# A two-layer f32 trunk on one core: all five engines in written order, seven split weight blocks, and a k-tile-major start

## The chip, the cores and the metric

The kernel runs on one core of one Trainium2 chip. The metric is the device time of one execution in microseconds, the median of several runs.

## The reference

The reference is a trunk of two layers over one sequence of 256 tokens with 1024 features, all in float32. Layer 0 mixes tokens by latent attention (MLA), layer 1 by forgetting attention (FoX). Cut to what matters:

```python
h = x
for i in range(2):
    h = h + 0.5 * swiglu(rms_norm(h, ffn_norm[i, 0]), ffn_w_in[i, 0], ffn_w_out[i, 0])
    u = rms_norm(h, mix_norm[i])
    h = h + (mla_mixer(u, ...) if i == 0 else fox_mixer(u, ...))
    h = h + 0.5 * swiglu(rms_norm(h, ffn_norm[i, 1]), ffn_w_in[i, 1], ffn_w_out[i, 1])
    gate = sigmoid(rms_norm(h, ple_norm[i]) @ ple_w_gate[i])
    h = h + gate * (p[i] @ ple_w_proj[i])
return rms_norm(h, final_norm)

def swiglu(x, w_in, w_out):          # w_in (1024, 2 * 2816), w_out (2816, 1024)
    gate, up = split(x @ w_in, 2, axis=-1)
    return (silu(gate) * up) @ w_out
```

## The kernel before, in words

Activations lie transposed: hT holds 1024 features as 8 k-tiles of 128 partitions by 256 tokens. Every large product is done in three reduced-precision products: each f32 operand is split into a high half and a low half (hi, lo), and hi·hi, lo·hi and hi·lo are summed. For a k-tile, PE runs one matmul with 512 columns (weight hi against activation hi and lo side by side, L228) and one with 256 (weight lo against activation hi, L229). Such a couple is called a pair in this text.

Weights come in blocks of 128 by 1024 (512 KB), one DMA each on SyncE's queue, into a buffer `raw`. For each half of 512 columns ScalarE writes `whi` (L97) and VectorE, in some stages POOL, subtracts to get `wlo` (L99). The class `Weights` keeps a plan of all blocks in order of use. `RAW`, `PAIRS` and `AHEAD` are the number of raw buffers, of split blocks, and how far the splits run ahead: 6, 5 and 4.

A `Norm` makes the operand of the next stage from hT: `scaled` writes the high half u on ScalarE (L270) and the low half on VectorE (L271), `square` and POOL's sum (L288) collect the norm's squares. The factor of each token comes later: `by_token` sums squares on PE (`pst`, L301), VectorE writes v (L304), POOL raises it to the power -0.5 (`rtok`, L306), VectorE multiplies the identity by it (`dg`, L311); `by_column` spreads it by a product (`pb`, L315), which ScalarE copies to `rb` (L317).

An FFN has 22 chunks of 128 hidden features. For each, a gate block (`pg`) and an up block (`pu`) of eight k-tiles go through PE; VectorE takes each out of PSUM times rb (`two`, L328), POOL adds its two halves (`gu`, L330), ScalarE does the silu (`sg`), POOL multiplies (`hid`, L334), and ScalarE and VectorE split that to `hs` (L208, L209). Then come eight output columns of 22 k-tiles each (`po`), and VectorE adds them to hT (L364). In the attentions, `fill` and `finish` interleave the output projection's columns (`ps`) with the last heads; the first four columns wait for the last head together, and `finish` adds a column to hT (L443) and hands it to the next norm. In FoX, POOL adds the halves of each projected query and key (L637). The position tables for MLA (`tables`, 41 small VectorE operations and two sines) are made during the first FFN. `ple` is the gated embedding at the end of each layer.

Seven PSUM banks are shared by all these products and one is kept for the norms.

The order of work: on PE and SyncE the instructions run in the order in which the program writes them. On the other three engines a planner orders them when the kernel is built, from its own costs and due times; on the chip each engine then runs its list in order, waiting at its head.

Of the kernel before, what the change touches and what calls it, by code (L numbers as in the profile page):

```python
# [61 lines left out]
class Weights:  # L62


    RAW, PAIRS, AHEAD = 6, 5, 4

    def __init__(self, nc, pool, plan, shared):
        self.nc, self.pool, self.plan = nc, pool, plan
        self.shared = shared
        self.got = self.loaded = self.fetched = 0  # L70
        self.live, self.raws, self.pairs = [], {}, {}

    def fetch(self):
# [6 lines left out]
    def load(self, pieces=1, between=None):  # L80
        nc = self.nc
        if pieces > 1:
            raw, src = self.fetch()
        else:
            while self.fetched < min(len(self.plan), self.loaded + self.RAW):
                nc.sync.dma_start(*self.fetch())
            raw = self.raws.pop(self.loaded)
        n = raw.shape[-1]
        hi = self.pool.tile([P, n], F32R, name="whi", bufs=self.PAIRS)
        lo = self.pool.tile([P, n], F32R, name="wlo", bufs=self.PAIRS)  # L90
        for i in range(pieces):
            c = slice(i * n // pieces, (i + 1) * n // pieces)
            if pieces > 1:
                nc.sync.dma_start(raw[:, c], src[:, c])
            for b in range(c.start, c.stop, 512):
                b = slice(b, min(b + 512, c.stop))
                nc.scalar.activation(hi[:, b], raw[:, b], AF.Copy)  # L97
                eng = nc.gpsimd if b.start and self.loaded in self.shared else nc.vector
                eng.tensor_sub(lo[:, b], raw[:, b], hi[:, b].bitcast(F32))  # L99
            if between:  # L100
                between(i)
        self.pairs[self.loaded] = (hi, lo)
        self.loaded += 1

    def ahead(self):
        oldest = min(self.live, default=self.got)
        while self.loaded < min(len(self.plan), self.got + self.AHEAD, oldest + self.PAIRS):
            self.load()

    def get(self, n=1):  # L110

        ids = list(range(self.got, self.got + n))
        self.got += n
        self.live += ids
        while self.loaded < self.got:
            self.load()
        self.ahead()
        return [(i, *self.pairs.pop(i)) for i in ids]

    def done(self, *ws):  # L120
        for w in ws:
            self.live.remove(w[0])
        self.ahead()
# [3 lines left out]
def trunk(ctx, tc, xT, pT, pos, gains, freq, bf, ffn_in, ffn_out, w_down, w_uq, w_ukv, mla_o,  # L127
# [13 lines left out]
    def plan_ffn(i):  # L141
        plan.extend(ffn_in[i, c] for c in range(2 * KF))
# [55 lines left out]
    def tmp(name):  # L198
        return work.tile([P, T], F32, name=name, tag="tmp", bufs=7)
# [54 lines left out]
    class Norm:  # L254
# [8 lines left out]
        def scaled(self, b, src, vector=False, cuts=(slice(0, T),)):  # L263
            g = g_sb[:, self.gain + b:self.gain + b + 1]
            hi, lo = self.pair[:, 0, b, :], self.pair[:, 1, b, :]
            for c in cuts:
                if vector:
                    nc.vector.tensor_scalar(hi[:, c], src[:, c], g, None, op0=ALU.mult)
                else:
                    nc.scalar.activation(hi[:, c], src[:, c], AF.Copy, scale=g)  # L270
                nc.vector.scalar_tensor_tensor(lo[:, c], src[:, c], g, hi[:, c].bitcast(F32),  # L271
                                               op0=ALU.mult, op1=ALU.subtract)

        def square(self, src, pool=False, cuts=(slice(0, T),)):
# [16 lines left out]
        def block(self, b, src, cuts=(slice(0, T),)):  # L291
            if self.gain is not None:
                self.scaled(b, src, cuts=cuts)
            self.square(src, cuts=cuts)

        def by_token(self, columns=True):
# [10 lines left out]
            if not columns:  # L307
                return
            self.dg = work.tile([P, 2, P], F32, name="dg", bufs=2)
            for t in range(2):  # L310
                nc.vector.tensor_scalar(self.dg[:, t, :], ident, self.rtok[:, t:t + 1], None, op0=ALU.mult)  # L311

        def by_column(self):
            pb = psm.tile([P, T], F32, name="pb", tag="small")
            nc.tensor.matmul(pb, ones, self.dg.rearrange("p a b -> p (a b)"), start=True, stop=True)  # L315
# [5 lines left out]
    def ffn(norm, nxt, meanwhile=None, at=1):  # L321
        hs = big.tile([P, 2, KF, T], F32R, name="hs", tag="big")

        def gate_up(c, ps):
            gu = []
            for p in ps:
                two = work.tile([P, 2, T], F32, name="two", tag="pair2", bufs=5)
                nc.vector.tensor_mul(two, p, norm.rb2)  # L328
                gu.append(tmp("gu"))
                nc.gpsimd.tensor_add(gu[-1], two[:, 0, :], two[:, 1, :])  # L330
            sg = tmp("sg")
            nc.scalar.activation(sg, gu[0], AF.Silu)  # L332
            hid = tmp("hid")
            nc.gpsimd.tensor_mul(hid, sg, gu[1])  # L334
            split(hs[:, 0, c, :], hs[:, 1, c, :], hid)

        ps0 = bank("pg"), bank("pu")
        blocks(ps0, norm.pair)
        waits = [(0, ps0)]
        for c in range(1, KF):  # L340
            pg = bank("pg")
            block(pg, norm.pair)
            if c == at:
                norm.by_token()
            pu = bank("pu")
# [3 lines left out]
            waits.append((c, (pg, pu)))  # L349
            if c >= at:  # L350
                for w in waits:
                    gate_up(*w)
                waits = []
            if c == 4 and meanwhile:
                meanwhile()
# [12 lines left out]
    def attention(project, score, v, scale, nxt, lag, fills, early, cumq=None):  # L368
# [4 lines left out]
        def scores(h):  # L373
# [15 lines left out]
            pr = work.tile([P, 3 * P], F32, name="pr", bufs=5)  # L389
            den = work.tile([P, 2], F32, name="den", bufs=3)  # L390
            nc.scalar.activation(pr[:, :P], ps[:, :P], AF.Exp, bias=nm[:, 0:1], scale=by[0], accum_out=den[:, 0:1])
            nc.scalar.activation(pr[:, P:], ps[:, P:], AF.Exp, bias=nm[:, 1:2], scale=by[1], accum_out=den[:, 1:2])
            inv = work.tile([P, 2], F32, name="inv", bufs=3)
# [3 lines left out]
            probs[h] = pr  # L397

        def turn(h):
            pr = probs.pop(h)  # L400
# [39 lines left out]
        def finish(d):  # L440
            W.done(ws[d])
            for p in parts(pss[d]):
                nc.vector.tensor_add(hT[:, d, :], p, hT[:, d, :])  # L443
            nxt.block(d, hT[:, d, :])

        for h in range(H + lag):
            if h < H:
# [8 lines left out]
            if h < H:  # L456
                project(h, 1)
            fill_some(fills.get((h, 1), 0))
# [17 lines left out]
    def mla(norm, nxt):  # L476
# [4 lines left out]
        norm.by_token()  # L481
        block(pkv, norm.pair, norm.by_column)
        nq = Norm(G_Q, 2, 2 * P, tag="q")
        for s in range(2):
            cq = tmp("cq")
            nc.vector.tensor_mul(cq, pq[s], norm.rb)
            nq.block(s, cq)
        nkv = Norm(G_KV, 1, P, tag="kv")
        ckv = tmp("ckv")
        nc.vector.tensor_mul(ckv, pkv, norm.rb)  # L490
        nkv.block(0, ckv)
# [424 lines left out]
```

## Time and profile before

| | |
|---|---|
| median of three runs | 1041.34 us (1040.74 to 1042.61) |
| profiled execution | 1040.49 us |
| span of its trace | 1038.7 us |
| granted clock of TensorE, mean | 0.991 |
| PE busy | 1003.6 us, 97% |
| VectorE (DVE) busy | 811.8 us, 78% |
| ScalarE (ACT) busy | 549.3 us, 53% |
| POOL busy | 409.3 us, 39% |
| DMA | 179.05 MB, mean 172 GB/s |

The span runs from the first to the last instruction; the execution's own time is 1.8 us longer. "Busy" is the share of the span in which an engine had an instruction in work; a matmul's end is modelled, so a busy PE can still run below its pace. In the list of waits, each row names the waiting instruction, the one that released it, the total in us, how often and the longest. In the list of groups, after the count stand busy us and the mean ns of one instruction, then the idle time ahead. A row of the table by stretches holds the busy time of PE, PEld, DVE, ACT and POOL with their counts of instructions, then the clock, the DMA share and GB/s. A row of the order of events holds start us, duration us, engine, line and what was made from what; in brackets the idle time before it and who ended it.

### The profile page before, as it was taken

To read this page: it belongs to the slowest core of one execution; us is meant where nothing else is said; L and a number is where in the kernel's file an instruction comes from. 1 tells how busy PE (TensorE), PEld (TensorE's weight loads), DVE (VectorE), ACT (ScalarE), POOL (GpSimd) and SP (SyncE) were. 2 spreads that over 40 slices of the span, in tenths; PEclk is the share of its full clock that TensorE was granted. 3 is DMA by queue.
4 is the path that set the end of the run, shared out by engine and by line. 5 is a ranking of instruction groups with operands and counts; after the bars stand their busy time and mean duration, and the time that the engine had idled before them with its cause. 6 is when DMAs were issued, how large, how long until landed. Compare 5 with 4: busy or idle time off the path is not lost. (4 is left out here: it accounts for less than half of the span.)

```text
span 1038.7 us, 17058 instructions
## 1 busy us (share of the span) xinstructions
PE 1003.6 (97%) x6084; PEld 888.0 (85%) x6084; DVE 811.8 (78%) x1367; ACT 549.3 (53%) x1168; POOL 409.3 (39%) x422
## 2 busy tenths in 40 slices
PE   6999999999979999999999999999999799999997
PEld 4888888987868888889888888899888688888896
DVE  8899987576669999766889997765766699997764
ACT  4445555466545554545655555556545455555554
POOL 4629531361326545110255552113664265551102
PEclk9999999999989999999999999999999899999998
DMA  7555666641345665665556656664443456656631
GB/s 274 186 195 159 187 205 199 204 143 61 92 158 180 201 184 185 193 198 166 187 177 202 186 179 181 196 207 149 143 152 113 161 169 198 193 180 194 195 119 42
DMA packets 51973, 179.05 MB, mean 172 GB/s; under 512 B 6064, under 2 KB 6960, under 8 KB 51888
## 3 DMA queue, kind: packets, MB, share of 16 engines
q1 hardware_dynamic: 50880, 176.48, 53.9%
q10 hardware_dynamic: 1008, 1.48, 0.4%
q8 instruction: 48, 0.79, 0.3%
q14 instruction: 37, 0.30, 0.1%
HBM read 176.89 MB, written 1.05 MB: 171 GB/s over the span
## 5 line engine op out<-in xcount | busy, mean ns | idle before, releaser
L99 DVE TENSOR_TENSOR wlo<-raw,whi 128x512 fp32r<-128x512 f32 (+1 forms) x646 | 472.3, 766 | 100.4 <-ACT whi L97 99.3
L97 ACT ACTIVATE whi<-raw 128x512 fp32r<-128x512 f32 (+1 forms) x688 | 382.7, 608 | 235.6 <-issue 81.9
L228 PE MATMUL pg<-u,whi 128*128 128x512 f32 x704 | 255.0, 400 | 20.0 <-DVE u L271 20.0
L228 PE MATMUL pu<-u,whi 128*128 128x512 f32 x704 | 254.3, 399 | 0.0
L330 POOL TENSOR_TENSOR gu<-two 128x256 f32<-128x256 f32 x176 | 169.0, 965 | 182.1 <-DVE two L328 165.8
L228 PE MATMUL po<-hs,whi 128*128 128x512 f32 x616 | 215.2, 393 | 0.9 <-DVE hs L209 0.9
L229 PE MATMUL pg<-u,wlo 128*128 128x256 f32 x704 | 199.9, 284 | 1.5 <-DVE wlo L99 1.5
L229 PE MATMUL pu<-u,wlo 128*128 128x256 f32 x704 | 199.9, 284 | 0.5 <-DVE wlo L99 0.5
L228 PEld LDWEIGHTS pg<-u,whi 128*128 128x128 f32 x704 | 133.4, 189 | 52.9 <-DVE u L271 14.8
L229 PE MATMUL po<-hs,wlo 128*128 128x256 f32 x616 | 173.3, 281 | 0.0
L228 PEld LDWEIGHTS pu<-u,whi 128*128 128x128 f32 x704 | 134.6, 191 | 30.7
L228 PEld LDWEIGHTS po<-hs,whi 128*128 128x128 f32 x616 | 115.7, 188 | 27.4 <-DVE hs L209 1.2
L229 PEld LDWEIGHTS pg<-u,wlo 128*128 128x128 f32 x704 | 133.7, 190 | 3.5 <-DVE wlo L99 3.4
L229 PEld LDWEIGHTS pu<-u,wlo 128*128 128x128 f32 x704 | 134.7, 191 | 1.0 <-DVE wlo L99 1.0
L208 ACT ACTIVATE hs<-hid 128x256 fp32r<-128x256 f32 x88 | 36.8, 418 | 165.3 <-POOL hid L334 165.3
L288 POOL TENSOR_TENSOR acc<-acc,sq 128x256 f32<-128x256 f32 x53 | 46.4, 876 | 187.3 <-ACT sq L280 186.6
L229 PEld LDWEIGHTS po<-hs,wlo 128*128 128x128 f32 x616 | 115.8, 188 | 0.0
L334 POOL TENSOR_TENSOR hid<-sg,gu 128x256 f32<-128x256 f32 x88 | 90.3, 1026 | 24.5 <-ACT sg L332 17.1
L99 POOL TENSOR_TENSOR wlo<-raw,whi 128x512 fp32r<-128x512 f32 x42 | 58.4, 1396 | 64.6 <-ACT whi L97 64.4
L209 DVE TENSOR_TENSOR hs<-hid,hs 128x256 fp32r<-128x256 f32 x88 | 58.7, 667 | 22.9 <-ACT hs L208 20.9
L328 DVE TENSOR_TENSOR two<-pg,rb 128x512 f32<-128x512 f32 x88 | 60.1, 683 | 8.7 <-PE pg L229 8.7
L328 DVE TENSOR_TENSOR two<-pu,rb 128x512 f32<-128x512 f32 x88 | 59.7, 678 | 0.3
(223 smaller groups left out, 1370.9 us busy)
## 6 DMA issues: line engine op xcount, KB each, us to landing
raw<-in_ffn_in_dram SPq DMA_DIRECT2D x174, 512.0 KB, 3.6
raw<-in_ffn_out_dram SPq DMA_DIRECT2D x64, 512.0 KB, 3.5
raw<-in_ffn_out_dram SPq DMA_DIRECT2D x32, 384.0 KB, 3.2
raw<-in_ple_gate_dram SPq DMA_DIRECT2D x16, 512.0 KB, 3.6
raw<-in_fox_qk_dram SPq DMA_DIRECT2D x16, 512.0 KB, 3.5
raw<-in_mla_o_dram SPq DMA_DIRECT2D x8, 512.0 KB, 3.5
raw<-in_fox_o_dram SPq DMA_DIRECT2D x8, 512.0 KB, 3.5
raw<-in_fox_v_dram SPq DMA_DIRECT2D x6, 512.0 KB, 3.4
```

Source lines behind the costliest of these rows:

```text
L97: nc.scalar.activation(hi[:, b], raw[:, b], AF.Copy)
L99: eng.tensor_sub(lo[:, b], raw[:, b], hi[:, b].bitcast(F32))
L208: nc.scalar.activation(hi, src, AF.Copy)
L209: nc.vector.tensor_sub(lo, src, hi.bitcast(F32))
L228: nc.tensor.matmul(ps, hi, x[:, :, k, :], start=k == 0, stop=False)
L229: nc.tensor.matmul(ps[:, 1, :], lo, x[:, 0, k, :], start=False, stop=k == last)
L288: nc.gpsimd.tensor_add(new, self.acc, sq)
L328: nc.vector.tensor_mul(two, p, norm.rb2)
L330: nc.gpsimd.tensor_add(gu[-1], two[:, 0, :], two[:, 1, :])
L334: nc.gpsimd.tensor_mul(hid, sg, gu[1])
```

## The change

All five engines run in the order in which the program writes them (`manual_schedule()` without a list), and the program is rewritten for that. Weight splits are written out at chosen places by `pump`, `catch_up` and `get`: ScalarE runs up to two blocks ahead of VectorE, and a block is split by one 1024-wide instruction per engine, or by two halves on VectorE and POOL for blocks in `shared`. There are seven split blocks and four raw ones, instead of five and six. The work of `Norm.block` is parted into `high`, `low` and `square`, with `last` for the last column, whose high half is made on VectorE. `dg` is gone: rtok, broadcast along its columns, is PE's weight and the identity its operand. The first four blocks of the first FFN come from a new array `ffn_first` by k-tiles: a slab has two k-tiles of all four blocks. Ahead of them PE runs 16 dummy products of zeros. The position tables are a generator that gives one step per half chunk of the first FFN. The `hs` split of a chunk follows the gate of the next chunk. In FoX the halves of a key are added on VectorE. The embedding's input is loaded and split during the FFN before it. `tmp` has 5 buffers instead of 7, `pair2` 4 instead of 5, `pr` 4 instead of 5.

```diff
-    RAW, PAIRS, AHEAD = 6, 5, 4
+    RAW, PAIRS = 4, 7
...
+    def fetch(self):
+        while self.fetched < min(len(self.plan), self.loaded + self.RAW):
+            self.nc.sync.dma_start(*self.raw())
...
+    def high(self, i, c):
+        self.nc.scalar.activation(self.pairs[i][0][:, c], self.raws[i][:, c], AF.Copy)
+
+    def low(self, i, c, eng=None):
+        hi, lo = self.pairs[i]
+        (eng or self.nc.vector).tensor_sub(lo[:, c], self.raws[i][:, c], hi[:, c].bitcast(F32))
+
+    def begin(self):
+        if self.begun < min(len(self.plan), min(self.live, default=self.got) + self.PAIRS):
+            hi, _ = self.pair()
+            self.high(self.begun - 1, slice(0, hi.shape[-1]))
+            return True
+
+    def pump(self, n=1):
+        for _ in range(n):
+            while self.begun < self.loaded + 2 and self.begin():
+                pass
+            if self.loaded == self.begun:
+                return
+            i = self.loaded
+            w = self.plan[i].shape[-1]
+            cut = 512 if i in self.shared else w
+            self.low(i, slice(0, cut))
+            if cut < w:
+                self.low(i, slice(cut, w), self.nc.gpsimd)
+            del self.raws[i]
+            self.loaded += 1
+            self.fetch()
+
+    def catch_up(self):
+        if self.loaded < self.got + self.PAIRS - 3:
+            self.pump()
...
+        def last(self, b, src):
+            self.high(b, src, True)
+            self.low(b, src)
+            self.square(src)
...
-            self.dg = work.tile([P, 2, P], F32, name="dg", bufs=2)
-            for t in range(2):
-                nc.vector.tensor_scalar(self.dg[:, t, :], ident, self.rtok[:, t:t + 1], None, op0=ALU.mult)
 
         def by_column(self):
             pb = psm.tile([P, T], F32, name="pb", tag="small")
-            nc.tensor.matmul(pb, ones, self.dg.rearrange("p a b -> p (a b)"), start=True, stop=True)
+            for t in range(2):
+                nc.tensor.matmul(pb[:, t * P:(t + 1) * P], self.rtok[:, t:t + 1].to_broadcast([P, P]), ident,
+                                 start=True, stop=True)
...
+        def gate(c, ps, pumps=1):
+            evacuate(c, 0, ps)
+            W.pump(pumps)
+            if c:
+                hidden(c - 1)
             sg = tmp("sg")
+            nc.scalar.activation(sg, gu.pop((c, 0)), AF.Silu)
+            gu[c, 0] = sg
+            next(meanwhile, None)
+
+        def up(c, ps, pumps=1):
+            evacuate(c, 1, ps)
+            hid[c] = tmp("hid")
+            nc.gpsimd.tensor_mul(hid[c], gu.pop((c, 0)), gu.pop((c, 1)))
+            W.pump(pumps)
+            if c % 2:
+                W.catch_up()
+            next(meanwhile, None)
...
+                for x, ps in enumerate(waits):
+                    gate(x, ps[0], x)
+                    up(x, ps[1], 0)
+                gate(c, pg)
+            up(c, pu, c > at)
         for d in range(KD):
...
+                if a + KD < KF:
+                    W.pump()
+                    next(meanwhile, None)
+                    if d == a == 0:
+                        hidden(KF - 1)
...
         def finish(d):
             W.done(ws[d])
+            src = hT[:, d, :]
             for p in parts(pss[d]):
-                nc.vector.tensor_add(hT[:, d, :], p, hT[:, d, :])
-            nxt.block(d, hT[:, d, :])
+                nc.vector.tensor_add(src, p, src)
+            if d == KD - 1:
+                nxt.last(d, src)
+                W.pump()
+                return
+            nxt.high(d, src)
+            if d < early and d:
+                nxt.low(d - 1, hT[:, d - 1, :])
+            if d >= early - 1:
+                W.pump()
+                nxt.low(d, src)
+            nxt.square(src)
...
-            nc.gpsimd.tensor_add(kq[:, 2 * h + half, :], two[:, 0, :], two[:, 1, :])
+            (nc.vector if half else nc.gpsimd).tensor_add(kq[:, 2 * h + half, :], two[:, 0, :], two[:, 1, :])
+            W.pump()
...
+    warm = const.tile([P, T], BF16, name="warm")
+    nc.vector.memset(warm, 0.0)
+    cold = bank("cold", (P, T))
+    for _ in range(16):
+        nc.tensor.matmul(cold, warm[:, :P], warm, start=True, stop=True)
+    for k in range(KD):
+        if k % 2 == 0:
+            W.pair()
+        n0.high(k, hT[:, k, :])
+        W.high(k // 2, half[k % 2])
+        n0.low(k, hT[:, k, :])
+        W.low(k // 2, half[k % 2])
+        n0.square(hT[:, k, :], pool=k % 2 == 1)
+        if k % 2:
+            W.loaded += 1
+
+    def first(ps):
+        W.fetch()
+        for k in range(0, KD, 2):
+            w, = W.get()
+            for j in range(2):
+                for i, p in enumerate(ps):
+                    part(p, w, n0.pair, range(k + j, k + j + 1), KD - 1, at=lambda x: (j * 4 + i) * P)
+            W.done(w)
+            W.pump()
...
-        with tc.manual_schedule(engines={mybir.EngineType.PE, mybir.EngineType.SP}):
+        with tc.manual_schedule():
```

In the embedding, `gated` makes the low half of the column before and pumps once between the sigmoid's input and the product with the gate. In MLA, the pumps stand behind `by_token`, behind `cr` (two), behind `turned`, behind each second half of `queries`, and behind the values (two).

More of the change, by code (lines that the diff above doesn't have):

```diff
@@ L78, in fetch @@
         return raw, src
[L80 to L108, printed above, removed]
+    def fetch(self):
+        while self.fetched < min(len(self.plan), self.loaded + self.RAW):
+            self.nc.sync.dma_start(*self.raw())
+    def pair(self):
+        n = self.plan[self.begun].shape[-1]
+        self.pairs[self.begun] = [self.pool.tile([P, n], F32R, name=x, bufs=self.PAIRS) for x in ("whi", "wlo")]
+        self.begun += 1
+        return self.pairs[self.begun - 1]
@@ L115, in get @@
         while self.loaded < self.got:
-            self.load()
-        self.ahead()
+            self.pump()
         return [(i, *self.pairs.pop(i)) for i in ids]
@@ L289, in square, with by_token @@
                 self.acc = new
[L291 to L296, printed above, removed]
+        def last(self, b, src):
+            self.high(b, src, True)
+            self.low(b, src)
+            self.square(src)
+        def by_token(self):
             pst = psm.tile([P, 2], F32, name="pst", tag="small")
@@ L348, in ffn @@
                 norm.by_column()
[L349 to L355, printed above, removed]
+                for x, ps in enumerate(waits):
+                    gate(x, ps[0], x)
+                    up(x, ps[1], 0)
+                gate(c, pg)
+            up(c, pu, c > at)
         for d in range(KD):
@@ L481, in mla @@
         norm.by_token()
+        W.pump()
         block(pkv, norm.pair, norm.by_column)
         nq = Norm(G_Q, 2, 2 * P, tag="q")
+        nkv = Norm(G_KV, 1, P, tag="kv")
+        cq = [tmp("cq") for _ in range(2)]
+        ckv = tmp("ckv")
         for s in range(2):
[L485 to L489, printed above, removed]
-        nc.vector.tensor_mul(ckv, pkv, norm.rb)
-        nkv.block(0, ckv)
+            nc.vector.tensor_mul(cq[s], pq[s], norm.rb)
+            nq.high(s, cq[s])
+        nc.vector.tensor_mul(ckv, pkv, norm.rb)
+        nkv.high(0, ckv)
+        for s in range(2):
+            nq.low(s, cq[s])
+            nq.square(cq[s])
+        nkv.low(0, ckv)
+        nkv.square(ckv)
         cr = work.tile([P, T], F32, name="cr", bufs=1, tag="c2")
         nc.vector.tensor_mul(cr, ck, norm.rb)
+        W.pump(2)
         block(pr, norm.pair)
@@ L530, in mla @@
             if hp == 1:
-                nq.by_token(False)
-                qscale = work.tile([P, 2], F32, name="qscale", bufs=1)
-                nc.vector.tensor_scalar(qscale, nq.rtok, MLA_SCALE, None, op0=ALU.mult)
+                nq.by_token()
+        W.done(w)
         nkv.by_column()
@@ L537, in mla @@
             nc.vector.tensor_mul(kT[:, 2 * i:2 * i + 2, :], pk[i], nkv.rb2)
-        W.done(w)
+        qscale = work.tile([P, 2], F32, name="qscale", bufs=1)
+        nc.vector.tensor_scalar(qscale, nq.rtok, MLA_SCALE, None, op0=ALU.mult)
         w, = W.get()
@@ L546, in mla @@
         W.done(w)
+        W.pump(2)
         def project(h, half):
```

256 lines of the change are left out of this document (166 added, 90 removed).

## The prediction

> **What bounds the kernel now.** I read the page first, then the waits of the TensorE queue, then the busy times by stretch, and last the order of events where PE stood still.
>
> ```profile
> span 1038.7 us, 17058 instructions
> ...
> PE 1003.6 (97%) x6084; PEld 888.0 (85%) x6084; DVE 811.8 (78%) x1367; ACT 549.3 (53%) x1168; POOL 409.3 (39%) x422
> ...
> PE   6999999999979999999999999999999799999997
> ...
> DVE  8899987576669999766889997765766699997764
> ```
>
> PE is the bound: it is full except in four slices, the first, the last, and two in between. So what a new order of the other engines can bring lies there. The waits of PE say for what it stood:
>
> ```profile
> PE pg L228 <- DVE u L271: 20.0, 10, 6.2
> PE pb L315 <- DVE dg L311: 2.2, 1, 2.2
> PE psc L641 <- POOL kqv L637: 2.2, 2, 1.3
> ...
> PE pst L301 <- ACT sq L280: 1.1, 1, 1.1
> PE po L228 <- DVE hs L209: 0.9, 1, 0.9
> ```
>
> Nearly all is one wait: the first FFN block needs u, the low half of the normed activations, from VectorE. The stretches show where (x counts matmuls):
>
> ```profile
> 0.00:20.00 20.00, 10.45 (x27) 6.64 (x28) 16.91 (x31) 9.34 (x18) 12.91 (x29) 1.00 0.75 260
> ...
> 284.00:300.00 16.00, 10.66 (x48) 8.44 (x47) 10.48 (x20) 5.57 (x12) 3.65 (x4) 0.79 0.43 132
> 300.00:418.00 118.00, 118.00 (x678) 103.55 (x678) 108.03 (x154) 62.60 (x129) 63.57 (x66) 1.00 0.60 186
> ...
> 508.00:516.00 8.00, 6.68 (x38) 5.62 (x38) 5.44 (x14) 4.62 (x13) 1.79 (x2) 1.00 0.48 151
> ...
> 804.00:820.00 16.00, 10.22 (x44) 8.15 (x44) 9.68 (x18) 4.66 (x11) 4.08 (x4) 0.79 0.42 132
> ...
> 1029.00:1039.00 10.00, 2.05 (x18) 1.74 (x16) 2.94 (x9) 2.87 (x8) 0.70 (x1) 0.71 0.27 105
> ```
>
> From 300 to 418 (gate and up products of the second FFN) nothing is lost: 118 us for 678 matmuls is 0.348 us for a pair (one hi, one lo), so 2.8 us for a block of eight k-tiles. At that pace 27, 48, 38 and 44 matmuls are worth 4.7, 8.4, 6.6 and 7.7 us, so the stretches lose 15.3 us at the start, 7.6 after the MLA mixer, 1.4 after the first embedding and 8.3 after the FoX mixer. With the 2.2, 2.2 and 0.9 us of the waits above, and 8 us in the last ten, that is 46 us.
>
> **The change, part by part.** Engine work hardly changes; order does. The sum is against the profiled execution: 1040.49 us, of which 1038.7 are the span; the median shown is 0.85 us above it.
>
> *Start.* Before, PE starts late and at a slow pace:
>
> ```profile
> 6.24 0.77 PE L228 MATMUL pg<-u,whi 128*128 128x512 f32 x1 [6.24 <-DVE u L271]
> ...
> 17.84 0.63 PE L228 MATMUL pu<-u,whi 128*128 128x512 f32 x1
> ...
> 18.48 0.63 PE L228 MATMUL pu<-u,whi 128*128 128x512 f32 x1
> ...
> 19.95 0.40 PE L228 MATMUL pu<-u,whi 128*128 128x512 f32 x1
> ...
> 20.30 0.39 PE L228 MATMUL pg<-u,whi 128*128 128x512 f32 x1
> ```
>
> A pair takes 0.64 us until 19 us and 0.35 after. By 20.30 fourteen pairs are done, worth 4.9 us: 15.4 lost. After, each k-tile feeds four blocks, 1.4 us of products, and VectorE has to give, per k-tile, one u and one 512-wide wlo. Their prices, and the others that I use:
>
> ```profile
> L99 DVE TENSOR_TENSOR wlo<-raw,whi 128x512 fp32r<-128x512 f32 x608 | 456.1, 783 | 100.4 <-ACT whi L97 99.3
> L328 DVE TENSOR_TENSOR two<-pg,rb 128x512 f32<-128x512 f32 x88 | 60.1, 683 | 8.7 <-PE pg L229 8.7
> L330 POOL TENSOR_TENSOR gu<-two 128x256 f32<-128x256 f32 x176 | 169.0, 965 | 182.1 <-DVE two L328 165.8 <-DVE st L778 12.1 <-ACT sg L332 2.2
> L99 POOL TENSOR_TENSOR wlo<-raw,whi 128x512 fp32r<-128x512 f32 x42 | 58.4, 1396 | 64.6 <-ACT whi L97 64.4
> L271 DVE SCALAR_TENSOR_TENSOR u<-hT,g_sb,u 128x256 fp32r<-128x256 f32 x63 | 49.5, 794 | 0.3 <-ACT u L270 0.2
> L443 DVE TENSOR_TENSOR hT<-ps,hT 128x256 f32<-128x256 f32 x30 | 11.4, 413 | 2.5 <-PE ps L229 2.5
> ```
>
> u 0.79 and wlo 0.78 make 1.6 us per k-tile, so VectorE sets this stretch. ScalarE queues its own table load ahead of its DMAs now, so g_sb may land 0.5 to 1 us later, but the 0.8 us in which VectorE made the high half of a second k-tile before the first u go: between 5.4 and 7.1 for the first product, and since the DMAs of ScalarE took only part of that path I take 5.5, the first wlo's end at 6.1. What is missed here is missed one for one. Seven more k-tiles end at 17.3, the last four pairs at 18.6; 32 pairs are worth 11.2, so 7.4 are lost: **gain 8.0** (9.5 if POOL, which has fewer squares, leaves VectorE free and PE's 1.4 sets the pace; 5.5 if a k-tile takes 1.9). DMA just covers it:
>
> ```profile
> raw<-in_ffn_in_dram SPq DMA_DIRECT2D x174, 512.0 KB, 3.6
> ```
>
> At the 260 GB/s of 0 to 20 us a block takes 2.0 of these 3.6 us, which leaves 1.6 of latency, and the 3.2 MB of slabs and input take 12.3: all is there near 14.6, and the last slab is wanted at 14.5. Each microsecond that it is later costs one. Sixteen dummies sit in idle time and cost nothing. The Trainium skill ("TensorE: Matmul & The Clock Gate", Part 1) says that the array runs at half rate until it was busy for about one free-running 3.4 us window; the trace agrees, with 0.64 against 0.35 us. By that rule sixteen 256-column dummies fill about one window and may miss it; then the first pairs run at 0.64, PE falls a k-tile behind and catches up at 0.2 us per k-tile, and the gain is at most 0.5 us smaller.
>
> *After the mixers.* Before, VectorE splits weights for later ahead of the residual that PE waits for:
>
> ```profile
> 272.04 1.10 DVE L443 TENSOR_TENSOR hT<-ps,hT 128x256 f32<-128x256 f32 x3 [0.92 <-PE ps L229]
> 273.06 0.68 DVE L99 TENSOR_TENSOR wlo<-raw,whi 128x512 fp32r<-128x512 f32 x1
> ...
> 277.74 2.27 DVE L99 TENSOR_TENSOR wlo<-raw,whi 128x512 fp32r<-128x512 f32 x2
> 279.93 0.47 DVE L271 SCALAR_TENSOR_TENSOR u<-hT,g_sb,u 128x256 fp32r<-128x256 f32 x1
> ...
> 281.06 1.22 DVE L99 TENSOR_TENSOR wlo<-raw,whi 128x512 fp32r<-128x512 f32 x1
> ...
> 288.96 0.74 DVE L443 TENSOR_TENSOR hT<-ps,hT 128x256 f32<-128x256 f32 x2
> ```
>
> ```profile
> 284.16 0.40 PE L228 MATMUL pg<-u,whi 128*128 128x512 f32 x1
> ```
>
> The last hT add ends at 289.7, though PE left the output projection at 284.2. After, finish() adds, then splits one block (pump), then makes u; the last column goes add, high, low ahead of its pump. What is late next: pump is first called at the fourth column, so the sixth o block (o5) is split behind four pairs of adds (0.74 each) and three lows (0.47), 0.68 for its first half: 5.1 us after 272.0, or 4.5 where starts overlap, while PE wants it three columns of 2.8 us ahead of 284.2, at 275.8: 0.7 to 1.3 us lost. The second FFN block is split after the last u, 2.5 to 2.9 us after PE's end, where PE has 2.45 us of the first: 0 to 0.5. Then only four blocks are ahead, and pu of the second pair waits about 1. I take 2.0 for 7.6 and 2.3 for 8.3: **gains 5.6 and 6.0** (ends: 7.6 and 8.3, if pumps find the lows already done; 2 each, if POOL's 1.4 us halves slow every VectorE operation). After the embedding only u of the column before and one pump lie between: 1.4 falls to 0.3, **gain 1.1**.
>
> *Mixers.* dg goes; rtok is itself PE's operand:
>
> ```profile
> 208.46 1.10 POOL L306 TENSOR_TENSOR rtok<-v,mhalf 128x2 f32<-128x2 f32 x1 [2.83 <-DVE v L304]
> ...
> 209.59 2.51 DVE L311 TENSOR_SCALAR dg<-ident,rtok 128x128 f32<-128x128 f32 x2 [0.60 <-POOL rtok L306]
> ```
>
> Before, dg ended at 212.1; rtok at 209.56 comes with PE's five k-tiles, so the 2.2 us go. But the second norm of MLA (nkv) now queues its v on VectorE behind tq and a pump, and its power on POOL behind three wlo halves of 1.4 and an add: about 1 us, where nothing was. **Gain 1.2** (2.2 to -0.5). In FoX every k add moves from POOL to VectorE: the waits on kqv go, **gain 2.0** (0 to 2.2). The two products with N=128 in by_column cost what one with 256 did; bounded by a pair, 0.35 us for each of nine norms if not, 3 us.
>
> *First FFN.* Per block of 2.8 us, VectorE is busy 108.03/118 x 2.8 = 2.56 now. One 1024-wide split instead of two 512-wide saves one start:
>
> ```profile
> 137.42 1.28 DVE L99 TENSOR_TENSOR wlo<-raw,whi 128x512 fp32r<-128x512 f32 x2
> ```
>
> Two take 1.28, pitch 0.60; one should take about 1.2, so 2.5 per block. But the position tables, 41 operations, are dealt out one per block:
>
> ```profile
> L778 DVE SCALAR_TENSOR_TENSOR ang<-turns,ang 128x256 f32<-128x256 f32 x5 | 2.5, 500 | 0.0
> ...
> L774 DVE TENSOR_SCALAR turns<-turns 128x256 f32<-128x256 f32 x3 | 0.9, 284 | 0.0
> ```
>
> 0.28 to 0.50 each, so 2.8 to 3.0: PE's own pace. VectorE enters this stretch late (six evacuations at 0.68, two splits, two hs lows and six table steps wait for the first rb: 8 to 10 us) and cannot catch up before the tables end. Seven pairs and seven banks cover that by about 1 us; I take 0.5 lost. At its end the last hs is queued behind that backlog and two pumps: 8 + 2.4 to 3 + 0.4 (the price of a hT add) = 11 us, and PE wants it after 21 pairs, 7.4: 3.5 lost, against 0.9. **Loss 3.1** (gain 0.9 without backlog; loss 8 if a step takes 0.1 more).
>
> *Elsewhere* the other gate and up stretches keep 0.3 us spare per block; SP, with four raw buffers, fetches each 8 us ahead of its split, against 3.6 us to landing (its bound: nothing). The tail keeps its chain: 0.
>
> Sum: 8.0 + 5.6 + 6.0 + 1.1 + 1.2 + 2.0 - 3.1 = 20.8. From 1040.49: 1019.7; with the 0.85 of the median, about 1020.5, and I say 1020.
>
> **The rivals.**
> *It goes cleaner.* VectorE keeps up through the tables, and all PE waits for u, dg, kqv and hs go: 9.5 + 7.6 + 8.3 + 1.4 + 2.2 + 2.2 + 0.9 = 32, so 1009. For it: VectorE did the tables before too, with PE at 9 in all those slices. Against it: the pump order above.
> *Given back in part.* The backlog in the first FFN grows (loss 8), the mixers' ends gain 3 each, the start 5.5, the rest 2: 5.5, so 1036; halfway to the forecast, 1028, is the middle of this case.
> *Slower.* In a fixed order VectorE waits at its head: for hs until POOL's product is there, for a wlo until ScalarE's whi is, with an evacuation behind it. It has 0.3 us spare per block. If such waits, or POOL's share of SBUF, add 0.4, VectorE becomes the bound at 2.9 in 168 blocks: 17 us lost, and with 0.45, 25 us, more than the forecast's gain: 1046. For it: beside POOL a wlo takes 1.22 us and alone 0.68 (both rows above), and the page shows DVE at 9 in these slices. Against it: seven banks and four blocks of lead absorb a wait that is not repeated. The Trainium skill ("GPSIMD Engine Reference", Specifications) states that GpSimd shares its SBUF interfaces with VectorE, in contention with operations that have two SBUF inputs; the trace agrees, for the evacuations, which read PSUM, have a mean of 683 ns.
> *No change.* The new order would have to lose at other places what it wins, 20 us, to within 2: unlikely.
>
> **How the numbers follow.** Forecast 0.53 (1013 to 1026), cleaner 0.2, given back in part 0.17, slower 0.06, no change 0.04. A measurement of this kernel tells 0.2%, about 2 us. The range leaves out slower, no change, half of the worst part of giving back and little of cleaner: 1008 to 1031. Faster: 0.53 + 0.2 + 0.17 = 0.90; same 0.04; slower 0.06.
>
> **What would show it.** Start: a first real product near 5.5 us, four-block pairs at VectorE's 1.6 us per k-tile, 32 done near 18.6. After the mixers: waits on u below 1 us, a short one on wlo of the o projection, no half-rate stretch. MLA: no wait for dg, one of about 1 us at the second pb. First FFN: VectorE at full until about 130 us, PE waiting for hs at its end. It is wrong if PE shows repeated short waits for wlo or banks inside gate and up, or if the start waits for slabs.

## The result, and the profile after

The changed kernel takes 1046.21 us (median of nine runs, 1044.17 to 1047.23). The kernel before, in nine runs beside it, takes 1042.61 us. The ratio is 1.0033, 95% interval 1.0022 to 1.0045: slower by a third of a per cent, where 1020 us were forecast. The profiled executions are not the medians: the changed kernel's took 1047.12 us, 0.9 above its median, and the one before 1040.49, 2.1 below the median beside it. So the spans below differ by 6.6 us where the medians differ by 3.6.

From the page of the changed kernel:

```profile
span 1045.3 us, 16475 instructions
...
PE 1011.7 (97%) x6118; PEld 894.2 (86%) x6118; DVE 759.7 (73%) x1057; ACT 515.4 (49%) x824; POOL 497.8 (48%) x410
...
PE   8999989999999999999899999999898999999997
...
PEclk8999989999999999999999999999999999999998
```

VectorE has 52 us less to do and POOL 88 us more. PE, still the bound, is now short of full in six slices instead of four. Its waits:

```profile
PE pu L246 <- DVE wlo L98: 5.4, 6, 2.2
PE ps L246 <- DVE wlo L98: 5.1, 2, 2.6
PE po L245 <- DVE hs L226: 3.9, 1, 3.9
PE ps L231 <- DVE wlo L98: 2.6, 3, 0.9
PE pt L465 <- DVE pr L458: 2.2, 2, 1.9
PE pg L245 <- DVE u L291: 2.0, 2, 1.8
PE psc L733 <- DVE kqv L728: 1.4, 1, 1.4
PE pg L246 <- DVE wlo L98: 1.2, 5, 0.3
```

The 20 us of waiting for u are down to 2.0. In their place PE waits 14.3 us (the four rows that end in wlo) for a weight's low half, where before there were 2.0:

```profile
PE pg L229 <- DVE wlo L99: 1.5, 2, 0.8
...
PE pu L229 <- DVE wlo L99: 0.5, 1, 0.5
```

The next table cuts the span where the first product of a stage starts, in the changed kernel and in the last of the kernels tried (e10 below). A gain is the length of the stretch before, less its length after.

| stretch | starts at, before | changed | e10 | forecast gain | gain, changed | gain, e10 |
|---|---|---|---|---|---|---|
| start and first FFN's gate and up | 0 | 0 | 0 | 7.5 | 4.7 | 5.4 |
| first FFN's output columns | 139.20 | 134.52 | 133.81 | -2.6 | -5.7 | 1.1 |
| MLA to its output projection | 201.98 | 202.97 | 195.51 | 1.2 | 1.6 | 1.6 |
| output projection, second gate and up | 255.81 | 255.22 | 247.75 | 5.6 | 1.4 | 6.1 |
| second FFN's output columns | 415.94 | 413.92 | 401.83 | 0 | -0.2 | -0.2 |
| embedding, third gate and up | 477.49 | 475.62 | 463.54 | 1.1 | -7.6 | -1.2 |
| third FFN's output columns | 632.28 | 637.97 | 619.56 | 0 | -0.2 | -0.2 |
| FoX to its output projection | 693.79 | 699.70 | 681.29 | 2.0 | -1.3 | 1.5 |
| output projection, fourth gate and up | 778.34 | 785.53 | 764.32 | 6.0 | 1.7 | 5.4 |
| fourth FFN's output columns to the end | 937.17 | 942.69 | 917.70 | 0 | -1.1 | -0.8 |
| sum | | | | 20.8 | -6.6 | 18.6 |

(The forecast's loss of 3.1 in the first FFN is parted into its two rows, 0.5 and 2.6.) Four stretches carry the miss; here is what PE did in each, in the order of events of the changed kernel.

**Start.**

```profile
2.76 1.91 PE L852 MATMUL cold<-warm 128*128 128x256 bf16 x8
6.47 0.47 PE L245 MATMUL pg<-u,whi 128*128 128x512 f32 x1 [1.80 <-DVE u L291]
```
```profile
5.30 0.51 ACT L286 ACTIVATE u<-hT,g_sb 128x256 fp32r<-128x256 f32 x1 [3.08 <-DMA g_sb<-in_gains_dram]
```

ScalarE's first u waits for the gains' DMA until 5.3, so the first product starts at 6.47. The dummies end 1.8 us before it. When the gains land differs between executions: in the traces of e1, e2, e3, e5 and e11 below, whose starts are the same, the first product comes between 6.29 and 8.39 us.

**End of the first FFN**, VectorE and then PE:

```profile
141.82 2.60 DVE L98 TENSOR_TENSOR wlo<-raw,whi 128x1024 fp32r<-128x1024 f32 x2
145.49 0.42 DVE L226 TENSOR_TENSOR hs<-hid,hs 128x256 fp32r<-128x256 f32 x1 [1.06 <-ACT hs L225]
```
```profile
145.97 0.80 PE L245 MATMUL po<-hs,whi 128*128 128x512 f32 x1 [3.94 <-DVE hs L226]
```

**End of the MLA mixer**, VectorE, POOL and PE:

```profile
275.76 0.54 DVE L291 SCALAR_TENSOR_TENSOR u<-hT,g_sb,u 128x256 fp32r<-128x256 f32 x1
276.23 1.76 DVE L98 TENSOR_TENSOR wlo<-raw,whi 128x512 fp32r<-128x512 f32 x1
```
```profile
275.98 1.45 POOL L98 TENSOR_TENSOR wlo<-raw,whi 128x512 fp32r<-128x512 f32 x1
```
```profile
275.06 0.40 PE L245 MATMUL ps<-os,whi 128*128 128x512 f32 x1
278.05 0.58 PE L246 MATMUL ps<-os,wlo 128*128 128x256 f32 x1 [2.59 <-DVE wlo L98]
```

The sixth block of the output projection is split after the adds and lows of the first columns. PE has used up the five blocks before it by 275.5 and stands.

**Embedding.** The lead shrinks in the same way: no block is split until the second column is done, and PE uses three by then. PE (the high half of the second row's block stood on ScalarE behind a u that waited for hT):

```profile
492.68 0.39 PE L231 MATMUL ps<-u,wlo 128*128 128x256 f32 x1 [0.86 <-DVE wlo L98]
...
497.35 0.39 PE L230 MATMUL ps<-u,whi 128*128 128x256 f32 x1 [0.95 <-ACT whi L94]
498.60 0.38 PE L231 MATMUL ps<-u,wlo 128*128 128x256 f32 x1 [0.87 <-DVE wlo L98]
...
500.19 0.41 PE L230 MATMUL ps<-u,whi 128*128 128x256 f32 x1
```

Behind these stops PE runs at half rate. The busy times by stretch (the figure after POOL is the granted clock; the fifth stretch lies behind the embedding's two stops of 0.95 and 0.87 us):

```profile
4.90:8.20 3.30, 1.56 (x7) 1.19 (x8) 1.18 (x2) 1.86 (x5) 0.47 (x1) 1.00 0.98 333
8.40:15.00 6.60, 6.13 (x19) 4.73 (x18) 6.52 (x9) 6.08 (x15) 5.07 (x6) 0.50 0.80 287
...
144.90:151.50 6.60, 5.53 (x17) 4.76 (x18) 5.81 (x8) 3.86 (x6) 0.11 (x1) 0.50 0.80 229
...
278.00:281.20 3.20, 3.15 (x10) 2.77 (x11) 2.91 (x5) 1.51 (x3) 2.00 (x2) 0.50 0.53 164
...
499.90:503.10 3.20, 3.20 (x17) 3.20 (x16) 1.39 (x4) 1.20 (x3) 0.72 (x1) 0.50 0.74 236
```

One more difference, in the groups (each shape by itself):

```profile
L98 DVE TENSOR_TENSOR wlo<-raw,whi 128x1024 fp32r<-128x1024 f32 x262 | 329.1, 1261 | 10.1 <-ACT whi L94 10.0
```
```profile
L348 POOL TENSOR_TENSOR gu<-two 128x256 f32<-128x256 f32 x176 | 252.6, 1436 | 120.9 <-DVE two L346 111.5
```

A block's split of 1024 columns costs VectorE 1.26 us, where two 512-wide ones of 0.783 were 1.57. POOL's addition of a product's two halves takes 1436 ns instead of 965.

### The profile page after: what moved, and what is told of

It is laid out like the page before. It is cut to its first block, busy times and chain, and to the rows that moved or that the text cites. A ratio compares the mean times of both kernels' runs of the same rounds, so it can differ in the third digit from the quotient of the medians.

```text
span 1045.3 us, 16475 instructions
## 1 busy us (share of the span) xinstructions
PE 1011.7 (97%) x6118; PEld 894.2 (86%) x6118; DVE 759.7 (73%) x1057; ACT 515.4 (49%) x824; POOL 497.8 (48%) x410
## 4 chain that ended last, share of the span: by engine, by line
PE 73%; DVE 15%; ACT 4%; POOL 3%; issue 3%; DMA 2%; SPq 0%; ACTq 0%; DVEq 0%; POOLq 0%
PE po L245 13%; PE pu L245 11%; PE pg L245 11%; PE po L246 7%; PE pu L246 6%; PE pg L246 6%; DVE wlo L98 6%; PE ps L245 4%; PE ps L246 2%; DVE two L346 2%; DVE hs L226 2%; PE ps L230 2%; PE ps L231 2%; PE ps L232 1%; POOL hid L367 1%
## 5 line engine op out<-in xcount | busy, mean ns | idle before, releaser
L98 DVE TENSOR_TENSOR wlo<-raw,whi 128x1024 fp32r<-128x1024 f32 (+1 forms) x346 | 412.4, 1201 | 15.8 <-ACT whi L94 14.7
L94 ACT ACTIVATE whi<-raw 128x1024 fp32r<-128x1024 f32 (+1 forms) x346 | 339.8, 1017 | 32.0 <-DMA raw<-in_ffn_in_dram 21.1
L348 POOL TENSOR_TENSOR gu<-two 128x256 f32<-128x256 f32 x176 | 252.6, 1436 | 120.9 <-DVE two L346 111.5
L245 PE MATMUL pg<-u,whi 128*128 128x512 f32 x704 | 252.2, 395 | 2.0 <-DVE u L291 2.0
L245 PE MATMUL po<-hs,whi 128*128 128x512 f32 x616 | 218.2, 397 | 3.9 <-DVE hs L226 3.9
L308 POOL TENSOR_TENSOR acc<-acc,sq 128x256 f32<-128x256 f32 x53 | 52.6, 993 | 185.8 <-ACT sq L300 185.4
L225 ACT ACTIVATE hs<-hid 128x256 fp32r<-128x256 f32 x88 | 36.8, 418 | 128.1 <-POOL hid L367 128.1
L286 ACT ACTIVATE u<-hT,g_sb 128x256 fp32r<-128x256 f32 x57 | 29.0, 509 | 141.5 <-DVE hT L411 112.2
L367 POOL TENSOR_TENSOR hid<-sg,gu 128x256 f32<-128x256 f32 x88 | 94.6, 1075 | 6.9
L226 DVE TENSOR_TENSOR hs<-hid,hs 128x256 fp32r<-128x256 f32 x88 | 70.8, 804 | 31.4 <-ACT hs L225 31.4
L411 DVE SCALAR_TENSOR_TENSOR hT<-po,hT 128x256 f32<-128x256 f32 x60 | 25.4, 424 | 82.8 <-PE po L246 71.9
```

Source lines behind the costliest of these rows:

```text
L94: self.nc.scalar.activation(self.pairs[i][0][:, c], self.raws[i][:, c], AF.Copy)
L98: (eng or self.nc.vector).tensor_sub(lo[:, c], self.raws[i][:, c], hi[:, c].bitcast(F32))
L225: nc.scalar.activation(hi, src, AF.Copy)
L226: nc.vector.tensor_sub(lo, src, hi.bitcast(F32))
L245: nc.tensor.matmul(ps, hi, x[:, :, k, :], start=k == 0, stop=False)
L286: nc.scalar.activation(self.pair[:, 0, b, c], src[:, c], AF.Copy, scale=g)
```

## The experiments

The theory was that the written places of the splits leave too few split blocks at the ends of stages, and that the rest of the loss is the tables in the first FFN. The rivals were that the order written out by hand is itself dear, that raw blocks come too late, that the wide split slows POOL, and that VectorE has too much to do in any order. Each kernel is the changed kernel with the edit shown; times are medians, ratios are to the kernel before on the same chip (1041.6 to 1041.9 us). The changed kernel's 1046.21 us was measured beside a kernel before of 1042.61, so up to 1 us of each difference to it is the occasion's.

**A split in the attentions' last heads (e1).**

```diff
             if h < H:
                 project(h, 1)
                 W.catch_up()
+            else:
+                W.pump()
```

> The changed kernel with one split more (pump) in each of the last iterations of the attentions, in which no head is projected (three in MLA, two in FoX); nothing else. Theory place: in the written order the sixth block of the output projection is split behind four pairs of residual adds, PE waits 2.6 and 2.5 us for its wlo, and falls to half rate for 3.4 us after each (1.6 us more); with the two extra splits both waits and both slow stretches go, and with two blocks more of lead most of the 1.5 us that the next FFN waits for wlo: 2 x (2.6 + 1.6 + 1) = 10 us, 1036. Rival supply: with four raw buffers the extra splits wait for their DMA and hold VectorE's queue; at most 3 us gained, 1043 or more. Rival contention: 1024-wide splits and POOL slow each other wherever they stand; within 2 us of 1046.

Measured 1039.99 us, ratio 0.9978 (0.9969 to 0.9988): 6.2 us below the changed kernel. Both waits for the sixth block go and the output projections fall from 32.6 to 28.3 and from 31.0 to 27.6 us. (1.5 us of the first is the half rate behind the wait; in the traces of e3 and e6 the same wait passes without it, and the projection takes 31.1.) It falls short of 1036 since a split now stands ahead of the last columns' u, where PE waits once more:

```profile
287.48 0.50 PE L245 MATMUL pg<-u,whi 128*128 128x512 f32 x1 [1.70 <-DVE u L291]
```

and since FoX's attention becomes 1.6 us longer: a stop of 1.9 us for the probabilities, which the changed kernel's trace also has, is followed there by 3 us of half rate.

**Splits after the embedding's first two columns (e2).**

```diff
             if d == 0:
                 norm.by_token()
+                W.pump()
             else:
                 if d == 1:
+                    W.pump()
                     norm.by_column()
```

> The changed kernel with one pump more behind each of the first two columns of both embeddings, where the written order has none until the norm is there. Theory place: the lead of split blocks runs out in the embedding of layer 0 (PE waits 0.9, 1.0 and 0.9 us for weights, 1.7 us of half rate follow, 2.2 us for the second block of the next FFN and about 1 us in its next blocks) and once 0.9 us in layer 1; these go: 8 us, 1038. Rival supply: no gain from splitting earlier, as the raw block is not there: 1044 or more. Rival contention: within 2 us of 1046.

Measured 1042.84 us, ratio 1.0005 (0.9995 to 1.0014): 3.4 us below the changed kernel, not 8. The embedding falls from 34.5 to 30.6 us. Two of its three waits are gone, one of 0.85 us is left, and no half-rate stretch follows; without one, the traces of e1 and e3, whose embeddings are unchanged, show 33.0 us. The wait of 2.1 us for the second block of the next FFN, which is split behind `last`, stays.

**The tables moved behind the first FFN's output columns (e3).**

```diff
-            next(meanwhile, None)
+            if c >= KF - 2:
+                next(meanwhile, None)
...
+                    for _ in range(3):
+                        next(meanwhile, None)
```

> The changed kernel with the position tables' steps given out in the output columns of the first FFN (three behind each pump, the first four in the last two chunks) instead of one per half chunk. Theory backlog: VectorE enters the first FFN late and the table steps keep it late to the end; without them it catches up 0.3 us per block, the last hs is in time, its 3.9 us wait and the 2 us of half rate behind it go: 6 us, 1040. Rival order: the two splits that stand ahead of the last hs on VectorE are what is late: then about 2 us of wait stay and 1042 to 1043 is seen. Rival supply: no change.

Measured 1039.51 us, ratio 0.9981 (0.9971 to 0.9990). The output columns take 61.7 us instead of 68.5: the wait for hs and the half rate behind it are gone. So the table steps were the backlog.

**Dummies up to the first product (e6).**

```diff
-    for _ in range(16):
+    for _ in range(34):
```

> The changed kernel with 34 dummy products instead of 16, so that they reach up to the first real one. In the changed kernel the clock record shows full rate from 4.9 to 8.3 us and half rate from 8.3 to 15.1. Theory gap: the idle 1.8 us between the last dummy and the first product let the clock fall; with 34 it stays. Then the start is bound by VectorE, whose last 512-wide wlo of the four slabs ended at 20.2 against 21.9 for PE: 0.5 us faster, 1045.7. Rival clock-bound: PE's half rate sets the start, 3.4 us faster, 1043.

Measured 1045.15 us, ratio 1.0043 (1.0026 to 1.0060); its interval overlaps that of the changed kernel. Its busy times by stretch:

```profile
4.90:8.20 3.30, 3.18 (x22) 2.51 (x21) 1.18 (x2) 1.38 (x4) 0.00 (x0) 1.00 1.00 333
8.40:15.00 6.60, 5.58 (x29) 4.06 (x27) 6.26 (x8) 6.39 (x15) 5.36 (x7) 1.00 0.76 266
```

The clock stays at 1.00 here, and so it does at the start of the three later kernels with 34 dummies (e8, e8b, e10). The gap is not the whole cause, though. Of the other traces with the same 16 dummies, those of e1 and e3 show 3 us of half rate behind the gap, e11's none behind a gap of 1.71 us, and in those of e2 and e5 the first pairs already run at 0.64 us. From the first product to the end of the four blocks e6 takes 15.3 us, e11 15.2, e5 15.2 and the changed kernel 15.4, whatever the clock (e2, which starts latest, 13.9): VectorE, not PE, set that stretch.

**All engines but PE and SyncE back to the planner (e4).**

```diff
-        with tc.manual_schedule():
+        with tc.manual_schedule(engines={mybir.EngineType.PE, mybir.EngineType.SP}):
```

> The changed program, with only PE and SyncE in written order and the other three engines ordered by the planner as before. Theory place: the waits come from the written order alone; the planner mixes splits and residuals by its own costs, keeps the better start (5 us) and has the waits for u after the mixers back: about 1038 to 1042. Rival contention or supply: the wide splits and the four raw buffers are still there, so 1046 or more.

Measured 1061.19 us, ratio 1.0184 (1.0169 to 1.0199): 15 us above the changed kernel. The ends of stages do improve (output projections by 4.3 us each, embedding by 4.9), but each gate and up stretch but one and each output stretch loses 3.4 to 5.5:

```profile
PE po L245 <- DVE hs L226: 15.0, 5, 4.7
PE pg L245 <- DVE u L291: 10.1, 6, 2.4
```

So the written order is not the loss; for this program it gains. Its weak places are those where the planner was better.

**Six raw and six split buffers (e5).**

```diff
-    RAW, PAIRS = 4, 7
+    RAW, PAIRS = 6, 6
```

> The changed kernel with six raw and six split blocks (the same memory) instead of four and seven; nothing else. Theory supply: where VectorE splits late, its raw block is freed late, the next DMA comes late, and VectorE and ScalarE stand at their heads for it (ScalarE waited 21 us for the FFN's blocks and 8 for FoX's); with six raw blocks these waits go, and with them the 3.6 us that PE stands in FoX and part of the embedding's: 4 us or more, 1042. Theory place: what is late is the split's place in the order; FoX gains at most 1.5 and one block less of lead costs as much elsewhere: 1045 to 1048.

Measured 1082.66 us, ratio 1.0398 (1.0382 to 1.0413). Both expectations miss by over 34 us.

```profile
PE ps L246 <- DVE wlo L98: 13.4, 5, 5.3
PE ps L231 <- DVE wlo L98: 10.6, 11, 1.5
PE pg L246 <- DVE wlo L98: 8.6, 8, 4.2
PE ps L230 <- ACT whi L94: 6.6, 2, 3.8
```

ScalarE's waits for the FFN's raw blocks, in the changed kernel and here:

```profile
ACT whi L94 <- DMA raw<-in_ffn_in_dram: 21.1, 14, 3.8
```
```profile
ACT whi L94 <- DMA raw<-in_ffn_in_dram: 3.2, 2, 2.2
```

So the raw blocks come in time now, and PE still waits more, nearly all for splits: supply of raw blocks is not the limit. Most of the loss lies in the first embedding (43.0 us for 34.5), in FoX's output projection (39.5 for 31.0) and behind the last FFN (50.2 for 40.9). One split block of lead is worth a great deal there. `catch_up` stops one block earlier with `PAIRS` too; which of the two it was is not separated.

**e1, e2, e3 and e6 together (e8).** The edit is the four diffs above.

> The three moves together (pumps in the last iterations of the attentions, pumps behind the first two columns of the embeddings, table steps in the output columns of the first FFN) and 34 dummies. Theory place: they act at different places, so their gains of 6.2, 3.4 and 6.7 us add up, with 0.5 for the dummies: 1046.2 - 16.8 = 1029.4. Rival one bound: VectorE gives back what it wins, 1036 or more.

Measured 1028.27 us, ratio 0.9875 (0.9860 to 0.9890): the losses are separate and their gains add up, as well as this can be told. In medians the sum is 16.8 us and 17.9 are measured; by the ratios it is 13.0 and 16.5, where each ratio's interval reaches 1 to 2 us to either side.

**The same, with the column's low half ahead of the split (e8b).**

```diff
-                W.pump()
                 nxt.low(d, src)
+                W.pump()
```

> As the run with all moves, and in the output projections' last five columns the low half of u is made ahead of the pump. With the extra pumps PE waited 1.7 us for u behind four splits at the start of the FFN. Theory place: that wait goes, and the splits still come in time, since two more blocks of lead are there: 2 x 1.7 us, and up to 1.6 us where half rate followed: 1026. Rival: the splits are then late by as much: within 1 us of the run with all moves.

Measured 1029.53 us, ratio 0.9885 (0.9866 to 0.9903), an interval that overlaps that of e8. The waits for u behind the mixers fall from 3.3 to 2.7 us, and a half-rate stretch appears at 501 us: the order of these two makes no difference that could be measured.

**Two splits at two places (e10), on top of e8.**

```diff
-            W.pump()
+            if c != 2:
+                W.pump(2 if c == 1 else 1)
...
-                W.pump()
+                W.pump(2 if d == KD - 3 else 1)
```

In FoX the split behind the last column of the values is written one column earlier; in the embedding one is added.

> The four edits together (a split in attention's last heads, splits after the embedding's first columns, table steps moved behind the first FFN's output columns, 34 dummies), and two splits instead of one at two places: in the embedding after the column third from the last, so that the second block of the next FFN is split ahead of the vector's last writes, and in FoX after the middle column, so that a split stands ahead of the gates chain. Theory that the written place of a split decides: the wait of 2.1 us for the second FFN block behind the embedding and FoX's waits (1.3 us for the k pieces, 3.1 us for the probabilities, and some 1.7 us of half rate) go in part, 1022 to 1026 us against 1028. Rival, that VectorE's amount of work ahead of these points decides and a split moved forward only pushes what stands behind it: 1027 to 1030 us, the same waits under other names.

Measured 1022.22 us, ratio 0.9811 (0.9793 to 0.9828), the best of all. Its page and waits:

```profile
span 1020.1 us, 16546 instructions
...
PE 1002.0 (98%) x6136; PEld 888.0 (87%) x6136; DVE 747.0 (73%) x1057; ACT 515.2 (51%) x824; POOL 495.5 (49%) x410
...
PE   9999999999999999999999999999999999999996
```
```profile
PE pg L245 <- DVE u L291: 3.3, 2, 1.7
PE pt L468 <- DVE pr L461: 1.9, 2, 1.2
PE ps L231 <- DVE wlo L98: 1.5, 2, 0.9
PE pg L246 <- DVE wlo L98: 1.4, 6, 0.4
...
PE pu L246 <- DVE wlo L98: 0.8, 1, 0.8
```

The wait for the second FFN block and the one for the k pieces are gone, and FoX up to its output projection takes 4.3 us less than in e8 (83.0 after 87.3). VectorE's amount of work is that of the changed kernel to 13 us of 760; what was changed is its place. That decides against the rival that VectorE has too much to do.

**VectorE's splits as two halves (e11).**

```diff
-            self.low(i, slice(0, cut))
+            self.low(i, slice(0, 512))
+            if cut == w > 512:
+                self.low(i, slice(512, w))
```

> The changed kernel with VectorE splitting each of its own blocks in two subtractions of 512 columns instead of one of 1024. Theory that the wide subtraction itself holds GpSimd back (its gate x up product took 1436 ns in the changed kernel, 965 before): the product is back under 1.1 us, the wait for hs in the first FFN (3.9 us) is a little shorter, 1041 to 1045 us. Rival, that any subtraction of VectorE beside it costs the same per column: the product stays at 1.35 to 1.45 us and the time within 2 us of 1046.

Measured 1050.62 us, ratio 1.0089 (1.0071 to 1.0108): 4.4 us slower.

```profile
L350 POOL TENSOR_TENSOR gu<-two 128x256 f32<-128x256 f32 x176 | 188.6, 1073 | 190.6 <-DVE two L348 186.5 <-ACT whi L94 1.6
```
```profile
L98 DVE TENSOR_TENSOR wlo<-raw,whi 128x512 fp32r<-128x512 f32 x608 | 507.6, 874 | 15.4 <-ACT whi L94 14.4 <-issue 0.9
```

Half of the theory holds. The 965 and 1436 ns that it gives to the gate x up product are those of POOL's addition of two halves (`gu`); that one is back at 1.07 us, so the wide form did hold it up. But VectorE pays 1.75 us for a block instead of 1.26, and in the first gate and up stretch, which becomes 6.1 us longer from its first product (134.2 after 128.1), it is busy for 102.8 of the 106 us from 24 to 130: VectorE is the bound there. The waits for hs at this FFN's end grow, from 3.9 to 6.4 us.

## Why the prediction was wrong

The term for the waits on u held: 20.0 us became 2.0. What failed are the terms for what is late next: they were too small or missing.

*Embedding, forecast +1.1, measured -7.6.* The step "only u of the column before and one pump lie between" looked at u alone. It didn't count blocks: PE uses three before the first pump (e2, with two pumps more, lost two of the three waits), and the second block of the next FFN is split behind the last u. The prediction had this very item after the mixers ("0 to 0.5") and not here; it was 2.2 us. This is the largest miss, 8.7 us.

*After the mixers, forecast +5.6 and +6.0, measured +1.4 and +1.7.* The place was right (the sixth block, behind adds and lows), its size wrong. I had it 0.7 to 1.3 us late. PE stood 2.6 us for it: its split was priced at 0.68 us and took 1.76 beside POOL's half, though the row of 1.22 us beside POOL stood in the prediction. And I priced a stop of PE at its length, where in this trace a half-rate stretch of 3.2 us follows. With the split moved (e1, in e10) these terms are 6.1 and 5.4.

*First FFN's end, forecast -2.6, measured -5.7.* The wait for hs came as worked out, 3.9 us for 3.5. Missing is the half-rate stretch behind it, which the sum puts at nothing: in 5.5 busy us PE did 17 matmuls, which are worth 3.0 us at 0.348 for two, so 2.5 us more are lost.

*FoX, forecast +2.0, measured -1.3.* Moving the k adds did not remove the wait on kqv (2.2 before, 1.4 after), and a new one for the probabilities (2.2) appeared: VectorE's fixed list puts both behind other work. A split written ahead of the gates (e10) brings +1.5.

*Start, forecast +7.5 with the first gate and up, measured +4.7.* The first product came at 6.47 instead of 5.5 (the gains' DMA, queued behind ScalarE's table load, landed at 5.3), and the four blocks were done at 21.9 instead of 18.6: from the first u at 5.84 to the last at 18.62 VectorE took 1.8 us for a k-tile, not 1.6, with one wait of 1.2 us for ScalarE in it. The half rate cost little here (e6). No run moved this part by itself.

*MLA, forecast +1.2, measured +1.6*: right. The wait for dg is gone; new ones of 0.5 us (for v) and 0.2 us (for rtok) stand where about 1 us was expected.

Of the rivals, the one that ended slower was not what happened. It made VectorE the bound inside gate and up; there PE runs full, with VectorE at less than I had assumed:

```profile
296.00:406.00 110.00, 108.98 (x626) 95.25 (x626) 87.20 (x101) 56.18 (x81) 79.75 (x61) 1.00 0.62 190
```

87.2 of 110 us are 2.2 us per block, 0.6 to spare instead of 0.3. I had let the wide split save the 0.08 us between 1.28, the price of two at one quiet place, and 1.2; in these stretches two had cost 2 x 0.836 = 1.67 us, and one wide one 1.25. That 1046 is also this rival's number is chance. What happened is "given back in part" carried past zero: several waits at the ends of stages, four of them with a half-rate stretch behind. That case was stopped at 1036 since each of its terms was bounded by engine time alone. That e10 comes out near the forecast does not make the forecast right. It shows that gains of about this size were there, and that 24 us (1046.2 less 1022.2) hung on five places in the program at which splits are written, the place of the tables and, least of all, the dummies.

By the rule of the Trainium skill ("TensorE: Matmul & The Clock Gate", Part 1) that the array runs at half rate until it was busy for a window of about 3.4 us, the sixteen dummies might miss the window, for at most 0.5 us. In the changed kernel they did not: its first pairs, from 7.33 us on, run at 0.35 us, and the half rate of 8.4 to 15.0 us follows the idle 1.8 us, which I had not weighed. In e2 and e5 the first pairs did run at 0.64 us. The bound held: with half rate or without, the four blocks took 15.2 to 15.4 us (under e6 above). The same part of the Trainium skill says that the array is back at half rate after at least one idle window of about 3.4 us. Here stops of 1.8 and 2.6 us were enough in some executions; the measurement decides. I did not ask at all what would follow the stops that I forecast myself.

The contention that the Trainium skill states ("GPSIMD Engine Reference", Specifications) showed the other way round than weighed inside gate and up: POOL got slower (965 to 1436 ns), while VectorE had time to spare. At the end of the MLA mixer it showed as weighed, in VectorE's 512-wide split of 1.76 us.

What stays open: the first embedding is still 1.2 us longer in e10 than before, and why one split buffer less costs 36 us (e5) is only followed to the waits. Whether a stop of 1 to 3 us is followed by half rate differs between executions, and no run here tells why.

## What to carry to other kernels

When an order is written out by hand, count at each stage's end how many prepared blocks the bound engine uses before the next one is made, as well as the wait you set out to remove; here splits written a column or a head earlier (e1, e2 and the two of e10) were worth some 15 us, where the rewrite without them lost 3.6. Price a stop of PE at its length, and add as a possible cost the half rate behind it (some 1.5 to 2.5 us here). Odd jobs dealt into a stage with no slack (here 41 table steps) belong in one where the engine idles.

## What the runs showed of the hardware

Half rate can follow a stop of PE far shorter than the 3 us or more that one half-rate stretch lasts, and whether it does differs between executions. The same stop of 2.6 us at the end of the MLA mixer was followed by half rate in the changed kernel (278.0 to 281.2 us) and in e2, and by full rate in e3, e5, e6 and e11. From e6:

```profile
276.85 0.39 PE L246 MATMUL ps<-os,wlo 128*128 128x256 f32 x1 [2.58 <-DVE wlo L98]
```
```profile
277.00:284.00 7.00, 7.00 (x46) 6.37 (x47) 6.90 (x12) 3.58 (x7) 5.14 (x5) 1.00 0.54 160
```

A stop of 1.7 us (e1, 287 us) passed without; so did one of 2.2 us in the changed kernel (515 us). Two of 0.95 and 0.87 us, with one product between them, were followed by it in the changed kernel (499.9 us), not in e1 and e3. All stops of 3.5 us and more, once the clock had been full, had half rate during them or behind them. So single stops of 1.8 to 2.6 us went both ways here, and no threshold can be read from them. At the start the half rate came late: PE ran at full rate until 8.2 us, 1.7 us after it had resumed. In the changed kernel's nine executions the mean granted clock goes with the time: it is 0.986 or 0.987 in the five of 1046.2 us and more, and 0.990 to 0.992 in the four of 1044.9 us and less.

One 1024-wide subtraction of two SBUF operands costs VectorE 1.26 us, with a 256-wide POOL addition at 1.44 us; as two 512-wide ones it costs VectorE 1.75 us, with POOL at 1.07. Between these two runs the engines trade time, and the wide form gives it to VectorE.
